# The gate and the embeddings' product of a decoder trunk, rearranged: another order of the seven gate products and of their banks, the residual added by accumulating transfers, and three quarters of the embeddings' product moved into the hand-ordered second phase

## The chip, the core and the metric

The kernel runs on one core of one Trainium2 chip. The metric is the device time of one execution in microseconds (us). Before the change the median of three executions is 2514.31 us (2514.18 to 2516.86).

## What is computed

One layer of a decoder trunk, all in float32, with 2048 tokens and a model width of 1024:

```python
u = rmsnorm(h, ln1_g);  proj = u @ w_in          # gated linear attention + short convolution
h = h + concat([o, y]) @ w_out
u2 = rmsnorm(h, ln2_g);  a, bb = split(u2 @ w_gate_upffn)
h = h + (silu(a) * bb) @ w_down                  # hidden width 2816
u3 = rmsnorm(h, ln3_g)
gate = sigmoid(u3 @ w_ple_gate)                  # 1024 x 1024
h = h + gate * (p @ w_ple_proj)                  # p: 2048 x 256, the "embeddings"
return rmsnorm(h, lnf_g)
```

The change touches the last three lines of the sum: the gate, and the product `p @ w_ple_proj`.

## The kernel before

**Arithmetic.** Each float32 operand of a product is split into a high part (a cast on ACT, line 161) and a low part (a subtraction on DVE, line 162). A product is three matmul passes: high x high, high x low, low x high (`PASSES`, `product` at line 143, matmul at line 147). A "cut" below is such a cast with its subtraction. The big products (up, down, gate) use a seven-product scheme in the manner of Strassen: a 2 x 2 block product is formed from seven products of sums of blocks, numbered 1 to 7, whose results are combined.

**First phase, `mixing_phase` (line 284).** Four blocks of 512 tokens, `NB` of them, each with `NT` = 4 tiles of 128 tokens. `block` (line 639) does norm, input projection, attention, convolution and, for two column halves `n` and four tiles `ti`, the output projection (`unit`). After the second half of each tile, `norm_to_ops` (line 219) forms the second norm, turns it (`tr`, line 202), copies the turned tile from PSUM on ACT (line 233), fetches four older operand blocks from HBM (line 231), forms the sums for the seven products with four subtractions on POOL (line 217) and stores them to `up_ops` (line 234). In this phase only PE's order is written by hand; the other engines' instructions are ordered by the scheduler. At its end stands `embedding` (line 699): first `load_U` (line 713) for the first four products of the next phase, which fetches their operands (line 268) and cuts them, then all of `p @ w_ple_proj`: `p` is turned in four blocks of 512 tokens (line 708), each followed by 8 products of 6 matmuls, whose results ACT copies from PSUM (line 726) and SP stores as 16 tiles `emb` (line 728).

**Second phase, `up_phase` (line 771).** Gate-up products, every engine in the order in which the code is written, from a table of due work that `run(g)` carries out (groups -6 to -1 are run before the first product, lines 864 to 867).

**Last phase, `last_phase` (line 947).** Also in written order. `stream` (line 1010) works through a list of jobs of two steps each; a step is 12 matmuls (line 1022). Raw operands `wr` and `mr` are loaded four jobs ahead (line 981) and cut into `wh` and `mh` two jobs ahead (lines 161 and 162). `then(n, fn)` puts work off by `n` steps. First comes `down` for two batches of 1024 tokens, then `gated(0)` and `gated(1)` (line 1161). All seven gate products take 4 steps each. SP issues all transfers in order, and each of them first waits for the transfer issued eight earlier and for its buffers. PSUM has four banks `ps0` and four `ps1`; a product either opens four banks of its own or goes on in those of an earlier one (`stream(..., on, ...)`).

In `gated` before: the order is 1, 6, 2, 5, 7, 3, 4. Product 1 is copied to `acc`, 6 is added to `acc` by DVE, 2 goes on in 1's banks, 3 in 5's and 4 in 7's. `onto` (line 1178) multiplies the gate by the embedding tile `pp` (buffer pool of 4, fetched by SP at line 1172) and adds it to the row `h`: the addition, in part also the multiplication, is on POOL (line 217). The rows `h` are loaded by SP (line 1153), three when the half begins and five at step 10. `finish` norms a row (squares on ACT at line 1060, the inverse root on POOL at lines 1064 and 1066, scaling on DVE at line 1079) and stores it (line 1185). In the last half product 4 is done token tile by token tile, with `last_done4` (line 1254): `early_half` multiplies by the norm's gain on POOL, and the scaled copies of `late_half` are on POOL (line 1211) for four tiles and on ACT (line 1209) for the other four.

Of the kernel before, what the change touches and what calls it, by code (L numbers as in the profile page):

```python
# [8 lines left out]
F32 = mybir.dt.float32  # L9
F32R = mybir.dt.float32r  # L10
# [28 lines left out]
def hybrid_layer(ctx: ExitStack, tc: tile.TileContext,  # L39
# [212 lines left out]
    def load_x(b, ti, eng, gate=None):  # L252
        xt = w4([P, D])
        r = b * T + ti * P
        d = eng.dma_start(out=xt, in_=x[r:r + P, :])
        if gate is not None:
            after(d, gate)
        return xt

# [24 lines left out]
    def mixing_phase(st):  # L284
# [354 lines left out]
        def block(b, u1, first):  # L639
# [7 lines left out]
            for n in range(2):  # L647
# [3 lines left out]
                for ti in range(NT):  # L651
# [10 lines left out]
                    unit(ps, uT_at(mix, tok_of(ti)), wo, NK, o_done)  # L662
            return u1
# [27 lines left out]
        pts = []  # L691

        def embedding_loads():
            for q in range(2):
                pts.append(w4([P, NT, 256]))
                r = slice(q * T, (q + 1) * T)
                nc.sync.dma_start(out=pts[q], in_=p[r, :].rearrange("(t p) d -> p t d", p=P))

        def embedding():
            wp = [weights(w_pp, [(n * 512, 512)], 0, 2) for n in range(2)]  # L700

            def turned(q):
                pT = [w4([P, 2, T], F32R) for _ in range(2)]
                for j in range(2):
                    tp = tr_bank().rearrange("p (k t) -> p k t", k=2)
                    for k in range(2):
                        for i in range(2):
                            nc.tensor.transpose(out=tp[:, k, i * P:(i + 1) * P],
                                                in_=pts[q][:, 2 * j + i, k * P:(k + 1) * P], identity=ident)
                    sl = slice(j * 256, (j + 1) * 256)  # L710
                    split_into(pT[0][:, :, sl], pT[1][:, :, sl], tp)
                return pT
            for n in ORDER[:4]:
                load_U(0, n, last["h"])
            pT = turned(0)
            for q in range(NB):
                if q + 2 < NB:
                    pts.append(w4([P, NT, 256]))
                    r = slice((q + 2) * T, (q + 3) * T)
                    nc.sync.dma_start(out=pts[q + 2], in_=p[r, :].rearrange("(t p) d -> p t d", p=P))  # L720
                for ti in range(NT):
                    o = w4([P, D])
                    for n in range(2):
                        ps = mm_bank()
                        product(ps, lambda k, s: pT[s][:, k, tok_of(ti)], wp[n], 2)
                        nc.scalar.copy(out=o[:, n * 512:(n + 1) * 512], in_=ps)
                        tick()
                    nc.sync.dma_start(out=emb[q * NT + ti], in_=o)
                    if ti == 1 and q + 1 < NB:
                        nxt = turned(q + 1)  # L730
                pT = nxt
# [39 lines left out]
    def up_phase(st):  # L771
# [175 lines left out]
    def last_phase(st):  # L947
# [14 lines left out]
        jobs = [(kind, b, n, i) for kind in range(2) for b in range(NBB) for n in ORDER  # L962
# [47 lines left out]
        def stream(kind, b, n, bk, on, done, by_token=False):  # L1010
            nk = kinds[kind][3]
            if on is None:
                tag = f"ps{flip[0] if n in (1, 7) else 1 - flip[0]}"
# [147 lines left out]
        def gated(b, lnf, final):  # L1161
            h = rows_of(h_out, b, 10)
            acc = [v("acc") for _ in range(NT)]
            bk, x22 = {}, [None] * NT
            part = [tiny.tile([P, 1], F32, name="part", bufs=2 * NT) for _ in range(2 * NT)] if final else None

            pp = {}

            def fetch(tiles, cols):
# [178 lines left out]
```

## Time and profile before

| | |
|---|---|
| median of three executions | 2514.31 us |
| the profiled execution | 2518.72 us |
| its span, first to last instruction | 2517.0 us |
| granted TensorE clock, mean | 0.979 |
| PE busy | 2388.6 us (95%) |
| DVE busy | 1405.2 us (56%) |
| ACT busy | 965.9 us (38%) |
| POOL busy | 775.1 us (31%) |
| moved by DMA | 470.03 MB, 187 GB/s in the mean |

The profiled execution is 4.41 us longer than the median, and 1.72 us of it lie around the span. The profile names an instruction by engine, line, operation and tiles ("mm<-hl,w" is a product into bank `mm` from `hl` and `w`). "Busy" is the sum of the durations. Behind an idle stretch stands in brackets its length and what released the engine: "[8.87 <-ACT mh L161]" is 8.87 us of waiting that a cast of `mh` on ACT ended. SPq is SP's queue of transfer issues, and "to landing" is the time from a transfer's issue until its data are there. Windows and timelines count in us from the span's start. The first phase ends and the second begins at about 1013 us, and the gate runs from about 2293 us to the end.

### The profile page before, as it was taken

The numbers are of one execution on the slowest core, as the hardware profiler recorded it, in microseconds if no ns is written. First come the engines' busy times: TensorE is split into PE (matmuls) and PEld (weight loads), VectorE is DVE, ScalarE is ACT, GpSimd is POOL, SyncE is SP. The second block draws the span as 40 slices with busy tenths as digits, with TensorE's granted clock in tenths as the row PEclk, the third lists the DMA queues.
The fourth block names the chain that finished last, engine by engine and source line by source line (L and its number), as shares of the span: only waits on it lengthen the run. The fifth ranks groups of instructions, "written<-read, shape, count | busy, mean of one in ns | idle before, by whom it ended". The sixth has DMA issues, their size and how long they took to land.

```text
span 2517.0 us, 31414 instructions
## 1 busy us (share of the span) xinstructions
PE 2388.6 (95%) x11752; PEld 1950.2 (77%) x11752; DVE 1405.2 (56%) x1662; ACT 965.9 (38%) x1511; POOL 775.1 (31%) x636
## 2 busy tenths in 40 slices
PE   7999999899999986999999999999999999999885
PEld 6777878777887765788888888888878887888664
DVE  4655465466537532555555754444546555656587
ACT  4434433353344324422222522222233354335454
POOL 3301211430103022334434144335413005303577
PEclk9999999999999998999999999999999999999888
DMA  4226323731442168635435666567677569658884
GB/s 152 67 68 225 95 68 143 221 107 61 167 126 76 60 205 296 222 135 179 159 134 184 221 250 217 194 225 259 234 246 242 190 225 358 207 198 291 296 306 162
DMA packets 273065, 470.03 MB, mean 187 GB/s; under 512 B 22528, under 2 KB 145936, under 8 KB 272912
## 3 DMA queue, kind: packets, MB, share of 16 engines
q1 hardware_dynamic: 272720, 468.00, 55.1%
q8 instruction: 92, 1.51, 0.2%
q14 instruction: 61, 0.50, 0.1%
q0 software_dynamic: 192, 0.02, 0.0%
HBM read 325.87 MB, written 142.08 MB: 186 GB/s over the span
## 4 chain that ended last, share of the span: by engine, by line
PE 66%; DMA 5%; POOL 3%; DVE 3%; ACT 2%; issue 1%; SPq 1%; DVEq 0%; POOLq 0%; ACTq 0%
PE mm L147 48%; PE ps L1022 16%; DMA mr<-u 1%; PE g L415 1%; DMA raw<-up 1%; DMA mr<-hid 1%; POOL h L217 1%; DVE mh L162 1%; DMA h<-h_out 0%; DMA wr<-in_w_ple_gate_dram 0%; DVE wh L162 0%; POOL w L217 0%; POOL as L217 0%; DVE g L217 0%; ACT mh L161 0%
## 5 line engine op out<-in xcount | busy, mean ns | idle before, releaser
L1022 PE MATMUL ps<-wh,mh 128*128 128x512 f32 x2520 | 592.5, 396 | 31.1 <-ACT mh L161 14.7
L1022 PEld LDWEIGHTS ps<-wh,mh 128*128 128x128 f32 x2520 | 478.8, 191 | 138.9 <-ACT mh L161 16.3
L147 PE MATMUL mm<-uT,hl 128*128 128x512 f32 x1920 | 481.8, 405 | 10.6 <-DVE hl L105 6.7
L147 PE MATMUL mm<-uT,wu 128*128 128x512 f32 x2112 | 482.7, 389 | 2.1 <-ACT wu L161 1.6
L147 PEld LDWEIGHTS mm<-uT,wu 128*128 128x128 f32 x2112 | 396.2, 188 | 85.2 <-ACT wu L161 2.1
L147 PEld LDWEIGHTS mm<-uT,hl 128*128 128x128 f32 x1920 | 356.8, 190 | 105.4 <-DVE hl L105 12.0
L147 PE MATMUL mm<-U,wu 128*128 128x512 f32 x1584 | 362.6, 389 | 0.0
L147 PEld LDWEIGHTS mm<-U,wu 128*128 128x128 f32 x1584 | 297.3, 188 | 61.7
L162 DVE TENSOR_TENSOR wu<-raw,wu 128x1024 fp32r<-128x1024 f32 x154 | 213.8, 1390 | 225.3 <-ACT wu L161 225.3
L147 PE MATMUL mm<-hl,uT 128*128 128x512 f32 (+1 forms) x1488 | 278.9, 347 | 3.4 <-DVE uT L162 2.1
L161 ACT CAST wu<-raw 128x1024 fp32r<-128x1024 f32 x154 | 161.3, 1049 | 307.2 <-PE mm L147 235.5
L162 DVE TENSOR_TENSOR wh<-wr,wh 128x1024 fp32r<-128x1024 f32 x112 | 149.2, 1332 | 224.7 <-ACT wh L161 224.6
L147 PEld LDWEIGHTS mm<-hl,uT 128*128 128x128 f32 x1488 | 235.2, 191 | 39.2 <-DVE uT L162 2.7
L217 DVE TENSOR_TENSOR v<-mm,v 128x512 f32<-128x512 f32 x220 | 151.3, 688 | 160.0 <-PE mm L147 159.2
L217 POOL TENSOR_TENSOR v<-v,v 128x512 f32<-128x512 f32 x88 | 139.9, 1590 | 303.1 <-DMA hid<-v 286.1
L161 ACT CAST wh<-wr 128x1024 fp32r<-128x1024 f32 x112 | 111.9, 999 | 272.2 <-PE ps L1022 186.9
L105 DVE TENSOR_TENSOR hl<-raw,hl 128x512 fp32r<-128x512 f32 (+1 forms) x260 | 183.3, 743 | 28.7 <-ACT hl L104 28.5
L104 ACT CAST hl<-raw 128x512 fp32r<-128x512 f32 (+1 forms) x260 | 154.0, 623 | 66.4 <-PE mm L147 34.2
L217 POOL TENSOR_TENSOR raw<-raw 128x1024 f32<-128x1024 f32 x44 | 106.1, 2423 | 217.6 <-issue 159.3
L162 DVE TENSOR_TENSOR mh<-mr,mh 128x1024 fp32r<-128x1024 f32 x112 | 153.9, 1374 | 6.6 <-ACT mh L161 6.3
L161 ACT CAST mh<-mr 128x1024 fp32r<-128x1024 f32 x112 | 111.5, 996 | 11.7 <-DMA mr<-hid 9.0
L217 POOL TENSOR_TENSOR ur<-ur 128x512 f32<-128x512 f32 x60 | 92.8, 1547 | 31.0 <-DMA ur<-in_w_ple_gate_dram 26.1
(173 smaller groups left out, 1968.0 us busy)
## 6 DMA issues: line engine op xcount, KB each, us to landing
raw<-in_w_gate_upffn_dram SPq DMA_DIRECT2D x77, 512.0 KB, 4.5
hid<-v SPq DMA_DIRECT2D x154, 256.0 KB, 3.4
mr<-hid SPq DMA_DIRECT2D x70, 512.0 KB, 4.8
raw<-in_w_in_dram SPq DMA_DIRECT2D x64, 512.0 KB, 4.6
wu<-raw SPq DMA_DIRECT2D x44, 512.0 KB, 2.8
raw<-wu SPq DMA_DIRECT2D x44, 512.0 KB, 5.7
wr<-wd SPq DMA_DIRECT2D x40, 512.0 KB, 3.7
w<-in_x_dram SPq DMA_DIRECT2D x32, 512.0 KB, 8.5
```

The lines of the kernel that those rows point to most:

```text
L104: nc.scalar.copy(out=hl[:, 0, :], in_=raw)
L105: nc.vector.tensor_tensor(out=hl[:, 1, :], in0=raw, in1=hl[:, 0, :].bitcast(F32), op=ALU.subtract)
L147: nc.tensor.matmul(out=out_ap, lhsT=lhs(k, a), rhs=rhs(k, b), start=(start and k == 0 and i == 0), stop=(k == nk - 1 and i == 2), **kw)
L161: nc.scalar.copy(out=hi, in_=src)
L162: nc.vector.tensor_tensor(out=lo, in0=src, in1=hi.bitcast(F32), op=ALU.subtract)
L217: return e.tensor_tensor(out=out, in0=a, in1=b, op=op)
L415: nc.tensor.matmul(out=sp[par][:, a, :], lhsT=X[r, c], rhs=X[r, c], start=True, stop=True)
L1022: nc.tensor.matmul(out=bk[n][t], lhsT=M[:, a, j, tok_of(t)], rhs=W[:, c, j, :], start=(on is None and k == 0 and i == 0), stop=(k == nk - ...
```

## The change

**Embeddings.** Only the first block of `p` (512 tokens) stays in the first phase. It is turned by `embedding_turned` behind the second tile of the last output projection, and its 8 products stand at the phase's end. The four `load_U` are gone from there. The other three blocks (24 products of 6 matmuls) stand at the start of the hand-ordered second phase: `p` is loaded into `ur` tiles, `w_ple_proj` is loaded and cut a second time (two transfers of 512 KB), and a table `events` puts the fetches and cuts of the operands of the first gate-up products, and the groups -6 to -1 of due work, between the 24 products. The results are stored as 24 transfers of 256 KB, each three products late.

**Gate.** The order is 1, 2, 6, 5, 7, 3, 4. Product 6 goes on in 1's banks, then 7 and 4 do too, and 3 goes on in 5's. 12 instead of 20 results are added up by DVE in each half, and product 4's sigmoid reads PSUM itself. In `gated(0)` `onto` is a single multiplication on DVE that writes `h`, and the old row is added by a transfer that POOL issues with `accum_op=add` (`residual`, eight of 512 KB); the squares come two steps after it. The embedding tiles come half in `pp` and half in `ut` buffers. In `gated(1)` all eight rows are loaded at step 8, and `onto`, `early_half` (both on DVE) and the scaled copies (on ACT) no longer use POOL. On POOL there remain the small inverses and the eight issues.

```diff
@@ embedding, first phase
+        def embedding_turned():
+            hi_lo = [w4([P, 2, T], F32R) for _ in range(2)]
+            turned_p(emb0["p"], lambda s, sl: hi_lo[s][:, :, sl], tr_bank)
...
-            for n in ORDER[:4]:
-                load_U(0, n, last["h"])
-            pT = turned(0)
-            for q in range(NB):
...
+            for ti in range(NT):
+                o = w4([P, D])
+                for n in range(2):
+                    ps = mm_bank()
+                    product(ps, lambda k, s: emb0["pT"][s][:, k, tok_of(ti)], emb0["w"][n], 2)
...
@@ up_phase
-        for g in range(-6, 0):
-            run(g)
-        load_U(0, ORDER[4])
-        side += fetch_U(0, ORDER[5])
+        for q in range(1, NB):
+            pts.append(pl["ur"].tile([P, 2, T], F32, name="ur"))
...
+        events = {0: lambda: (fetch_next(0), run(-6), run(-5), run(-4)), 3: lambda: (cut_all(), fetch_next(1)),
...
+                    events.get(u, lambda: None)()
+                    ps = mm_bank()
+                    product(ps, lambda k, s: pT(q)(k, s)[:, tok_of(ti)], lambda k, s: wpp[:, 2 * n + k, s, :], 2)
+                    o = v2()
+                    nc.scalar.copy(out=o, in_=ps)
...
@@ last_phase
-        jobs = [(kind, b, n, i) for kind in range(2) for b in range(NBB) for n in ORDER
+        orders = [ORDER, (1, 2, 6, 5, 7, 3, 4)]
+        jobs = [(kind, b, n, i) for kind in range(2) for b in range(NBB) for n in orders[kind]
...
@@ gated
+                if not final:
+                    tensor(V, row(t)[:, cols], sg, pp[t, cols.start], ALU.mult)
+                    return
+                tensor(V, sg, sg, pp[t, cols.start], ALU.mult)
+                tensor(V, h[t][:, cols], h[t][:, cols], sg, ALU.add)
...
             def finish(t, start):
-                norm_steps(h[t], lnf, start, (1, 2), lambda got: then(start + 3, lambda: store(t, got["xn"])))
+                def residual():
+                    nc.gpsimd.dma_start(out=h[t], in_=h_out[b * 2 * NT + t], accum_op=ALU.add)
+                then(start, residual)
+                norm_steps(h[t], lnf, start + 2, (1, 2), lambda got: then(start + 5, lambda: store(t, got["xn"])))
...
-                tensor(G, h[t][:, cols], h[t][:, cols], lnf[:, cols], ALU.mult)
+                tensor(V, h[t][:, cols], h[t][:, cols], lnf[:, cols], ALU.mult)
...
             def done4(t, x):
-                z = v("g")
-                tensor(V, z, x, acc[t], ALU.add)
-                then(1, lambda: sigmoid(z, z))
-                then(2, lambda: onto(t, hi, z, V, G))
-                finish(t, 4 + t)
+                z = v("acc")
+                sigmoid(x, z)
+                then(1, lambda: onto(t, hi, z))
+                then(1, lambda: finish(t, 2 + t))
...
+            if final:
+                then(8, lambda: [row(t) for t in range(2 * NT)])
+            then(1, lambda: fetch(early, lo, "pp"))
+            go(1, None, done1)
+            go(2, None, done2)
+            go(6, 1, done6)
             go(5, None, done5)
-            go(7, None, done7)
+            then(1, lambda: fetch(late, hi, "ut"))
+            then(3, lambda: fetch(late, lo, "pp"))
+            go(7, 1, done7)
+            then(1, lambda: fetch(early, hi, "ut"))
             go(3, 5, done3)
...
+            go(4, 1, last_done4 if final else done4, by_token=final)
```

**ACT at the end of the first phase, before.** `w<-tr` is the copy of a turned tile of the second norm, `uT<-raw` a cast of an operand for the next phase, and `w<-mm` the copy of a result of the embeddings' product.

```order
L178 ACTIVATE w_7932,ss<-w_7574 128x1024
L233 COPY w_7940<-tr 128x512 x2
L161 CAST w_8018<-tr 128x2x256 x2
L161 CAST uT<-raw 128x2x512 x6
L726 COPY w_8036<-mm 128x512
L161 CAST uT<-raw 128x2x512
L726 COPY w_8036<-mm 128x512
L161 CAST uT<-raw 128x2x512
L233 COPY w_8053<-tr 128x512 x2
L726 COPY w_8080<-mm 128x512 x2
L161 CAST w_8098<-tr 128x2x256 x2
L726 COPY w_8114<-mm 128x512 x2
```

**The same place after.** `U_8133` to `U_8135` hold the split blocks of `p` and `w_ple_proj` in the second phase.

```order
L178 ACTIVATE w_7962,ss<-w_7574 128x1024
L233 COPY w_7970<-tr 128x512 x2
L722 COPY w_7996<-mm 128x512 x2
L233 COPY w_8013<-tr 128x512 x2
L722 COPY w_8040<-mm 128x512 x2
L722 COPY w_8058<-mm 128x512 x2
L722 COPY w_8076<-mm 128x512 x2
L161 CAST U_8134<-raw 128x2x512 x2
L161 CAST U_8133<-mm 128x2x256 x4
L161 CAST U_8135<-mm 128x2x256 x2
L900 COPY v_8203<-mm 128x512
L900 COPY v_8212<-mm 128x512
```

The eight casts `uT<-raw` stood ahead of the copies of the last turned tile and are now behind them, among the 24 later copies.

**SP at the same place, before:** the stores of the last tile's sums (`up`), the loads of `p` and the stores of `emb`.

```order
L268 DMA raw<-up_5_105 128x1024 x2
L720 DMA w_8034<-in_p_dram 128x4x256
L231 DMA w_8054<-up_1_109 128x4x128
L231 DMA w_8054<-up_2_111 128x4x128
L728 DMA emb_196<-w_8036 128x1024
L234 DMA up_3_114<-w_8053 512x1x128
```

**SP after:**

```order
L234 DMA up_4_115<-w_8014 512x1x128
L724 DMA emb_196<-w_7996 128x1024
L724 DMA emb_197<-w_8040 128x1024
L724 DMA emb_198<-w_8058 128x1024
L724 DMA emb_199<-w_8076 128x1024
L862 DMA ur<-in_p_dram 128x4x256 x3
L866 DMA raw<-in_w_ple_proj_dram 128x2x512 x2
L279 DMA ur<-up_1_102 128x1024 x2
```

The loads of `p` for the second block of tokens stood ahead of the last stores of the first phase, and those of the last three blocks now stand behind the last tile's stores and behind the four stores of `emb`.

**POOL in `gated(0)`, before:** row additions (`h<-h,g`, `h<-h,x`) and multiplications (`g<-g,pp`), then the small inverses.

```order
L217 TENSOR_TENSOR g<-g,pp 128x512
L217 TENSOR_TENSOR h<-h,g 128x512
L217 TENSOR_TENSOR h<-h,x 128x512 x4
L217 TENSOR_TENSOR h<-h,g 128x512 x4
L1064 TENSOR_SCALAR ms<-ss_18227 128x1
L1066 TENSOR_TENSOR rs<-ms,mhalf 128x1
L1064 TENSOR_SCALAR ms<-ss_18254 128x1
```

**POOL after:**

```order
L1246 DMA h<-h_out_90 128x1024
L1246 DMA h<-h_out_91 128x1024
L1246 DMA h<-h_out_92 128x1024
L1106 TENSOR_SCALAR ms<-ss_18250 128x1
L1108 TENSOR_TENSOR rs<-ms,mhalf 128x1
L1246 DMA h<-h_out_93 128x1024
L1106 TENSOR_SCALAR ms<-ss_18296 128x1
```

POOL's row work is gone, and the transfers of the residual stand in POOL's queue among the inverses.

More of the change, by code (lines that the diff above doesn't have):

```diff
@@ L258, in load_x, with turned_p @@
         return xt
+    def turned_p(src, dst, bank):
+        for j in range(2):
+            tp = bank().rearrange("p (k t) -> p k t", k=2)
+            for k in range(2):
+                for i in range(2):
+                    nc.tensor.transpose(out=tp[:, k, i * P:(i + 1) * P],
+                                        in_=src[:, 2 * j + i, k * P:(k + 1) * P], identity=ident)
+            sl = slice(j * 256, (j + 1) * 256)
+            split_into(dst(0, sl), dst(1, sl), tp)
     U = [{}, {}]
@@ L662, in block @@
                     unit(ps, uT_at(mix, tok_of(ti)), wo, NK, o_done)
+                    if not more and n == 1 and ti == 1:
+                        embedding_turned()
             return u1
@@ L688, in start @@
                         fill_mask(L)
-        pts = []
+        emb0 = {}
         def embedding_loads():
[L694 to L697, printed above, removed]
-        def embedding():
[L700 to L712, printed above, removed]
-            for n in ORDER[:4]:
-                load_U(0, n, last["h"])
-            pT = turned(0)
-            for q in range(NB):
[L717 to L731, printed above, removed]
@@ new lines, in up_phase, with pT @@
+        for n in range(2):
+            nc.sync.dma_start(out=wpp_raw[n], in_=w_pp[:, n * 512:(n + 1) * 512].rearrange("(k p) n -> p k n", p=P))
+        spare2 = [pl["U2"].tile([P, 4, 2, T], F32R, name="U2") for _ in range(3)]
+        wpp = spare2[1]
+        for n in range(2):
+            split_into(wpp[:, 2 * n:2 * n + 2, 0, :], wpp[:, 2 * n:2 * n + 2, 1, :], wpp_raw[n])
+        def pT(q):
+            t = spare2[0 if q < 3 else 2]
+            return lambda k, s: t[:, (q - 1) % 2 * 2 + k, s, :]
@@ new lines, in up_phase @@
+        stores = []
+        u = 0
+        for q in range(1, NB):
+            for ti in range(NT):
+                for n in range(2):
+                    events.get(u, lambda: None)()
[3 more added lines that the diff above has]
+                    nc.scalar.copy(out=o, in_=ps)
+                    stores.append((emb[q * NT + ti][:, n * 512:(n + 1) * 512], o))
+                    if len(stores) > 2:
+                        nc.sync.dma_start(out=stores[0][0], in_=stores[0][1])
+                        stores.pop(0)
+                    u += 1
@@ L868, in up_phase @@
+        for d, o in stores:
+            nc.sync.dma_start(out=d, in_=o)
+        side += cuts
         for b in range(NBB):
@@ L1223, in done5, with done6 @@
+            def done6(t, x):
+                u2[t] = v("g")
+                nc.scalar.copy(out=u2[t], in_=x)
             def done5(t, x):
-                x22[t] = v("x")
-                tensor(V, x22[t], x, acc[t], ALU.add)
+                p5[t] = v("x")
+                nc.scalar.copy(out=p5[t], in_=x)
             def done7(t, x):
-                tensor(V, x22[t], x, x22[t], ALU.add)
-                then(1, lambda: sigmoid(x22[t], x22[t]))
-                then(2, lambda: onto(NT + t, hi, x22[t], V, G))
@@ L1231, in done7 @@
[L1231 to L1232 removed]
+                z = p5[t]
+                tensor(V, z, x, z, ALU.add)
+                then(1, lambda: sigmoid(z, z))
+                then(2, lambda: onto(NT + t, hi, z))
                 if final:
[L1234 removed]
+                    then(3 + t // 2, lambda: early_half(NT + t, hi))
             def done3(t, x):
[L1237 to L1238 removed]
+                z = u2[t]
```

126 lines of the change are left out of this document (71 added, 55 removed).

## The prediction

> **What bounds the kernel now.** I read the page first, then the waits of PE, then the windows, then the timelines of the two stretches that the windows single out. The page's busy times:
>
> ```profile
> span 2517.0 us, 31414 instructions
> PE 2388.6 (95%) x11752; PEld 1950.2 (77%) x11752; DVE 1405.2 (56%) x1662; ACT 965.9 (38%) x1511; POOL 775.1 (31%) x636
> ```
>
> PE is busy for 95% of the span. The change leaves the number of matmuls as it is, so what it can gain lies in PE's 128 us of idle time (2517.0 - 2388.6) and in matmuls that run slowly behind a stall. The windows show where these lie (PE busy and its count, ..., clock, DMA share, GB/s):
>
> ```profile
> 900.00:950.00 50.00, 40.10 (x184) 31.85 (x182) 18.14 (x22) 15.11 (x26) 18.29 (x20) 0.93 0.57 173
> 950.00:1000.00 50.00, 32.27 (x146) 26.62 (x147) 12.54 (x13) 24.54 (x39) 12.13 (x7) 0.80 0.88 301
> 1050.00:1100.00 50.00, 50.00 (x222) 41.38 (x222) 29.91 (x30) 13.86 (x17) 22.73 (x12) 1.00 0.50 168
> 2300.00:2350.00 50.00, 48.25 (x226) 39.34 (x225) 29.91 (x23) 24.38 (x34) 36.20 (x24) 1.00 1.03 348
> 2350.00:2400.00 50.00, 36.02 (x139) 27.61 (x137) 34.04 (x31) 18.97 (x24) 22.55 (x15) 0.86 0.77 258
> 2400.00:2450.00 50.00, 40.26 (x148) 30.97 (x149) 42.59 (x34) 27.52 (x40) 33.20 (x25) 0.86 0.87 316
> 2450.00:2517.00 67.00, 37.66 (x164) 30.34 (x162) 52.29 (x51) 29.94 (x56) 49.97 (x39) 0.82 0.47 176
> ```
>
> An undisturbed stretch (1050 to 1100) runs 222 matmuls in 50 us, or 0.225 us each; that is my full rate. The boundary of the first two phases and the gate fall well below it, and both are what the change touches.
>
> **The boundary.** PE's timeline there:
>
> ```profile
> 932.16 1.14 PE L708 MATMUL tr<-ident,w 128*128 128x128 f32 x8 [1.56 <-ACT w L233]
> 933.53 0.73 PE L147 MATMUL mm<-hl,w 128*128 128x512 f32 x2 [0.23 <-ACT w L161]
> 940.36 3.99 PE L147 MATMUL mm<-hl,w 128*128 128x512 f32 x10 [6.09 <-DVE w L162]
> 967.73 1.97 PE L708 MATMUL tr<-ident,w 128*128 128x128 f32 x8 [19.74 <-ACT w L233]
> 1012.62 0.73 PE L147 MATMUL mm<-uT,wu 128*128 128x512 f32 x2 [1.62 <-ACT wu L161]
> 1013.88 1.42 PE L147 MATMUL mm<-uT,wu 128*128 128x512 f32 x5 [0.52 <-DVE wu L162]
> ```
>
> Idle in all: 1.56 + 0.23 + 6.09 + 19.74 + 1.62 + 0.52 = 29.8 us. The long one ends with a copy on ACT (L233). ACT's own timeline says why that copy is late:
>
> ```profile
> 946.23 1.05 ACT L161 CAST uT<-raw 128x1024 fp32r<-128x1024 f32 x1 [12.26 <-DMA raw<-up]
> 966.15 1.05 ACT L161 CAST uT<-raw 128x1024 fp32r<-128x1024 f32 x1 [1.70 <-DMA raw<-up]
> 967.10 1.07 ACT L233 COPY w<-tr 128x512 f32<-128x512 f32 x2
> ```
>
> ACT stood in the casts of the next phase's operands, eight of them from 946 to 967, each waiting for its transfer, and the copy that frees PE's `tr` bank stood behind them.
>
> **The gate.** Its 2 x 7 x 4 x 12 = 672 matmuls, counted back from the last one in PE's timeline, begin 13 matmuls into its first row, at 2292.7, and the second half begins 22 matmuls into the fifth, at 2390.2:
>
> ```profile
> 2289.78 24.87 PE L1022 MATMUL ps<-wh,mh 128*128 128x512 f32 x109
> ...
> 2362.46 19.08 PE L1022 MATMUL ps<-wh,mh 128*128 128x512 f32 x73 [8.87 <-ACT mh L161]
> ...
> 2384.47 12.28 PE L1022 MATMUL ps<-wh,mh 128*128 128x512 f32 x47 [1.71 <-DVE mh L162]
> ...
> 2416.51 0.80 PE L1022 MATMUL ps<-wh,mh 128*128 128x512 f32 x1 [4.01 <-DVE wh L162]
> ...
> 2480.26 9.36 PE L1022 MATMUL ps<-wh,mh 128*128 128x512 f32 x40 [1.72 <-DVE mh L162]
> ```
>
> PE ends at 2480.26 + 9.36 = 2489.6. So the halves take 97.5 and 99.4 us where 336 matmuls at full rate are 75.6, and the tail to 2517.0 takes 27.4. The waits are for cuts. Cuts are late for two reasons, which SP's waits (in 2240 to 2517), the lines by form (from 2290) and DVE's timeline show:
>
> ```profile
> SPq L1172 <- DVE x L217: 22.3, 8, 10.0
> SPq L1172 <- DVE g L217: 19.6, 8, 7.0
> ```
>
> ```profile
> L162 DVE TENSOR_TENSOR mh<-mr,mh 128x1024 fp32r<-128x1024 f32 x27 | 45.8, 1695 | 1.4 <-ACT mh L161 1.3
> L162 DVE TENSOR_TENSOR wh<-wr,wh 128x1024 fp32r<-128x1024 f32 x27 | 43.3, 1603 | 40.8 <-ACT wh L161 40.8
> L217 POOL TENSOR_TENSOR h<-h,g 128x512 f32<-128x512 f32 x20 | 35.4, 1788 | 15.4 <-DVE g L217 14.7
> ```
>
> ```profile
> 2469.95 1.22 DVE L162 TENSOR_TENSOR mh<-mr,mh 128x1024 fp32r<-128x1024 f32 x1
> 2477.92 2.29 DVE L162 TENSOR_TENSOR mh<-mr,mh 128x1024 fp32r<-128x1024 f32 x1
> ```
>
> First, the embedding fetches wait 42 us in SP's queue for `pp` buffers, and the raw loads stand behind them. Second, a cut takes DVE 1.22 us while POOL is idle (2469.95) and 2.29 while POOL adds rows (2477.92). The Trainium skill, page "SBUF — State Buffer", section "SBUF: two separate sides", says the same of its cause: an exclusive lock on a port pair, which a DVE operation with two SBUF inputs and a GpSimd operation that reads SBUF take in turns. The trace agrees, 2.29 against 1.22.
>
> **The change part by part.** Durations are of the profiled execution (2518.72 us, span 2517.0, 1.72 around it), which is 4.41 us over the median; I take the differences from it and put them on the median.
>
> *Boundary.* The casts of operands go behind the copies. The last turned tile's own norm still holds PE for about as long as the first three stalls, some 5 to 8 us, and the first block's products end at about 950. Then the path is SP: the second block of `p` is issued behind the stores of the last tile, whose sums on POOL come one tile every 10.5 us:
>
> ```profile
> 932.37 2.61 POOL L217 TENSOR_TENSOR w<-w,w 128x512 f32<-128x512 f32 x2 [4.50 <-DMA w<-up]
> ...
> 942.87 2.63 POOL L217 TENSOR_TENSOR w<-w,w 128x512 f32<-128x512 f32 x2 [4.48 <-DMA w<-up]
> 946.71 1.29 POOL L217 TENSOR_TENSOR w<-w,w 128x512 f32<-128x512 f32 x1
> ```
>
> At that pace the last tile's sums run from 953.4 and take 5.1 us (946.71 + 1.29 - 942.87) to 958.5, and `p` is issued at about 959. The landings over the whole kernel were
>
> ```profile
> w<-in_p_dram SPq DMA_DIRECT2D x4, 512.0 KB, 9.2
> raw<-in_w_ple_proj_dram SPq DMA_DIRECT2D x2, 512.0 KB, 7.4
> ```
>
> so `p` is there at 968 and turned and cut two or three us later; 144 matmuls at 0.225 are 32.4 us, 34 with a slow start, which gives 1004 to 1005 for the first up product against 1012.6: **-8 us**. The table adds two transfers of the weight, and ACT has the eight casts among its 24 copies; eight `mm` banks of 6 matmuls (8 x 1.35 = 10.8 us) cover those. Bounds: +2 if the loads come 10 us later, -14 if SP is not held by the last tile.
>
> *First half of the gate.* The eight row loads leave it: 4.2 MB, at the 348 GB/s of the saturated window 12 us of transfer. The waits for `pp` go, POOL's row work goes, and the cuts fall from 1.6 to 1.7 us towards 1.22. Of the 21.9 us over full rate some are turns of the last norm, which stay. The 8.87 stall is the one I count, since it stands behind the saturated stretch: **-8**, bounds 0 and -15.
>
> *Residual.* Eight accumulating transfers come in. No row of before shows one. The nearest are the same rows by SP, and three small transfers issued by POOL:
>
> ```profile
> h<-h_out SPq DMA_DIRECT2D x16, 512.0 KB, 6.9
> cw<-in_conv_w_dram POOLq DMA_DIRECT2D x3, 2.0 KB, 3.5
> ```
>
> The squares come two steps (24 matmuls, 5.4 us) later. From 3.5 us up to 13.8 (twice 6.9, if the old row is read and then written) both an early and a late landing are open. I take 7: 1.5 us late, hidden by cuts that are two jobs (10.8 us) ahead. Their 4.2 MB lie in the second half. The Trainium skill, page "DMA: Bandwidth & Descriptors", section "Anatomy of one DMA", fits 2.0 us + bytes/436e3 to a transfer that GpSimd issues, for 512 KB an estimate of 3.2 us; no run here shows it, and the same rows by SP took 6.9. By it the squares would never wait and the sum would stay as it is.
>
> *Second half.* DVE loses 8 additions but takes `onto` and `early_half` from POOL, 24 row operations of 512 columns: at half of a cut's 1.22 us for 1024 columns some 15 us, against 54 cuts in both halves that each lose up to 0.4 us. All eight rows are asked for at step 8, next to stores and the residual, in a half that moved 258 and 316 GB/s in the windows and has the 348 of the first as a measure of room: (348 - 258) x 50 + (348 - 316) x 50 = 6.1 MB, against the 4.2 MB that come. The 23.8 us over full rate shrink by the `pp` waits and shorter cuts, and some stalls for rows appear: **-8**, bounds +8 and -18.
>
> *Tail.* POOL's end, from its timeline:
>
> ```profile
> 2486.02 6.34 POOL L217 TENSOR_TENSOR h<-h,g 128x512 f32<-128x512 f32 x4
> ...
> 2499.35 3.52 POOL L1211 TENSOR_SCALAR w<-h,rs 128x512 f32<-128x512 f32 x2
> ...
> 2503.91 4.15 POOL L1211 TENSOR_SCALAR w<-h,rs 128x512 f32<-128x512 f32 x2
> ```
>
> Additions to 2492.4, then inverses, then scaled copies to 2508: all but the inverses leave POOL. After the last matmul there remain sigmoid, multiplication, addition, squares, inverse and scaling of one tile, about 6 us, and its store, while eight stores (4.2 MB at 348 GB/s, 12 us) begin a little before PE's end: 13 of 27.4 remain, **-14**, bounds -6 and -17.
>
> Sum: -8 - 8 - 8 - 14 = -38 us, so 2514.3 - 38 = 2476 (the profiled execution would be 2481).
>
> **The rivals.**
>
> *The boundary gives nothing.* ACT's casts have only moved among the 24 copies. If operands land late there, in a stretch that already moved 301 GB/s in 950 to 1000 and gets two transfers more, banks fill and PE waits as now. Against it: the fetches are now three products (4 us) ahead of the casts, and the eight banks stand behind that. It gives -30: 2484.
>
> *The gate stays bound by its transfers.* The bytes of the gate are the same, only later, and the burst of rows at step 8 holds DVE (its `onto` waits for a row, with cuts queued behind). For it: 348 GB/s in 2300 to 2350 with a DMA share of 1.03. Against it: the windows behind that one are below. Both halves then give nothing, -8 - 14 = -22: 2492.
>
> *Slower: late residuals.* On POOL's queue the fourth residual stands behind the first row's inverse, which waits for squares, which wait for the first residual; so three are under way at a time. With a landing of L the rows come L/3 apart, where steps are 2.7 us, and ACT stands in the squares ahead of its casts. Over eight rows PE loses 8 x (L/3 - 2.7) + (L - 5.4) less the 10.8 us of cuts ahead: at L = 13.8, 13 us, which leaves 2489; at L = 20 some 35, which eats the gain; at 25 about 53, which gives 2530. It decides from L = 20, three times the 6.9 of SP's rows. For it: the operation has no row here, and it falls into the stretch where SP's own stores bunch. Against it: that factor.
>
> *The change does not do what it says.* PE's matmuls are the same in number, and if the stalls were set by PE's order alone nothing would move: 2514. Against it stand ACT's casts and POOL's rows above, both visibly ahead of what PE waits for.
>
> **How the numbers follow.** Forecast 0.62; boundary without gain 0.13; gate bound by transfers 0.12; late residuals 0.10; no effect 0.03. A measurement of this kernel can tell about 0.2%, 5 us, from no change. All of the first three are faster by more; of late residuals 0.08 are slower by more and 0.02 in between: faster 0.87, same 0.05, slower 0.08. The terms' bounds reach from 2514.3 - 14 - 15 - 18 - 17 = 2450 up, but will not all fall on one side; two thirds of the way down from the forecast is 2459. Above, the range takes in the second rival, 2492, with some of its own spread: 2502. Left out are the late residuals, no effect and about 0.05 at the ends.
>
> **What would show it.** Right: no wait of PE on ACT L233 above 7 us around 950, the first up product near 1004; cuts in the gate near 1.22 to 1.3 us; PE's end at about 2462 to 2466 and a tail of 12 to 14 us. Wrong: squares on ACT released by the residual's transfer with waits over 8 us; DVE's `onto` released by `h<-h_out`; a wait of PE at 950 that is as long as before and only ends with `p`; a tail over 20 us.

## The result and the profile after

The changed kernel takes 2490.27 us (median of four, 2487.02 to 2492.85) against 2515.59 us for the kernel before: the ratio is 0.9897, with a 95% interval from 0.988 to 0.9914. That is faster by 1.0%, as forecast, and inside the forecast range, but by 25 us and not by 38. One execution of the run "rows by SP" below took 8366 us and is left out of its median.

The span of the profiled execution fell from 2517.0 to 2488.0 us. Its pieces follow from PE's timeline, by counting the gate's 672 matmuls back from the last one as the prediction did (the middle of the gate falls inside a row of many matmuls and is taken there in proportion; the starts of the single matmuls would move it by 0.6 to 0.7 us in these two kernels and by at most 1.5 in the runs below, from one half to the other):

| us | before | after | difference | forecast |
|---|---|---|---|---|
| first up product | 1012.6 | 1008.5 | -4.1 | -8 |
| beginning of the gate | 2292.7 | 2285.8 | -6.9 | |
| first half of the gate | 97.5 | 85.8 | -11.7 | -8 |
| second half | 99.4 | 99.3 | -0.1 | -8 |
| tail, PE's end to the span's end | 27.4 | 17.1 | -10.3 | -14 |

In the runs below that share the changed kernel's code up to that point, the first up product came between 1003.6 and 1009.7 us, so the first two rows are good to a few us; the halves and the tail repeat within some 2 us where their code is the same. The pieces add up to 29.0 us and not to 25.3, since the profiled execution of the kernel before lay 3.1 us above its median and that of the change 0.6 below.

**The boundary** in PE's timeline of the changed kernel:

```profile
940.40 1.94 PE L202 MATMUL tr<-ident,w 128*128 128x128 f32 x8 [3.88 <-DVE w L195]
941.99 10.61 PE L147 MATMUL mm<-hl,w 128*128 128x512 f32 x36
964.67 5.35 PE L266 MATMUL mm<-ident,ur 128*128 128x128 f32 x24 [12.07 <-DMA ur<-in_p_dram]
971.80 0.73 PE L147 MATMUL mm<-U,U 128*128 128x512 f32 x2 [1.77 <-ACT U L161]
1008.49 6.74 PE L147 MATMUL mm<-uT,wu 128*128 128x512 f32 x29
```

The wait of 19.74 us for a copy behind ACT's casts is gone. In its place PE waits 12.07 us for `p`. The wait that ends last before the products is a shorter one for ACT, which had waited for the weight:

```profile
969.09 2.17 ACT L161 CAST U<-raw 128x1024 fp32r<-128x1024 f32 x2 [15.87 <-DMA raw<-in_w_ple_proj_dram]
971.16 3.02 ACT L161 CAST U<-mm 128x512 fp32r<-128x512 f32 x6
```

The casts of the weight stand ahead of those of the turned `p`, so the weight, which landed at about 969, holds the products at least as much as `p`. From the first of their 144 matmuls to the first up product 36.7 us pass.

**The gate.** PE's timeline shows one long wait in the second half; ACT's timeline shows what it stood in:

```profile
2390.44 5.29 PE L1064 MATMUL ps<-wh,mh 128*128 128x512 f32 x22 [0.63 <-DVE mh L162]
2405.58 1.22 PE L1064 MATMUL ps<-wh,mh 128*128 128x512 f32 x2 [9.86 <-ACT mh L161]
2461.55 9.36 PE L1064 MATMUL ps<-wh,mh 128*128 128x512 f32 x40 [0.63 <-DVE mh L162]
```

```profile
2378.24 1.06 ACT L1102 ACTIVATE w<-h 128x1024 f32<-128x1024 f32 x1 [5.21 <-DMA h<-h_out]
2402.50 1.06 ACT L1102 ACTIVATE w<-h 128x1024 f32<-128x1024 f32 x1 [10.31 <-DMA out_dram<-w]
2404.49 1.04 ACT L161 CAST mh<-mr 128x1024 fp32r<-128x1024 f32 x1
```

The squares of the first row waited 5.21 us for its residual. Those of a later row waited 10.31 us for the store that had to leave its output buffer, and the cast that PE needed stood behind them. The windows (with the clock, the DMA share and the GB/s at the end) and the DMA view from 2375 to 2425 us show what made that store late:

```profile
2330.00:2380.00 50.00, 47.73 (x201) 38.72 (x202) 35.66 (x37) 24.40 (x32) 11.54 (x9) 0.97 1.00 321
2380.00:2430.00 50.00, 36.22 (x141) 27.78 (x140) 32.40 (x34) 26.31 (x42) 14.24 (x20) 0.88 1.00 322
```

```profile
q1 hardware_dynamic: 3397, 11.35, 59.5%
q0 software_dynamic: 1088, 3.93, 40.6%
...
out_dram<-w SPq DMA_DIRECT2D x7, 512.0 KB, 10.1
h<-h_out POOLq DMA_DIRECT2D x5, 512.0 KB, 8.7
...
pp<-emb SPq DMA_DIRECT2D x4, 256.0 KB, 17.2
```

The DMA engines are full for 100 us. The queue of POOL's transfers (q0), the residuals, takes 40.6% of their time for 3.93 MB, which is 10.3% for each MB; SP's queue (q1) takes 59.5% for 11.35 MB, or 5.2% for each MB. Behind it an embedding tile of 256 KB takes 17.2 us to land.

DVE's cuts, in the lines by form from 2285 us on, did get faster, to 1.37 to 1.38 us from 1.60 to 1.70, with POOL's own row work for the gate gone:

```profile
L162 DVE TENSOR_TENSOR mh<-mr,mh 128x1024 fp32r<-128x1024 f32 x27 | 37.2, 1380 | 0.2
L162 DVE TENSOR_TENSOR wh<-wr,wh 128x1024 fp32r<-128x1024 f32 x27 | 37.0, 1370 | 51.9 <-ACT wh L161 51.9
```

**The tail.** DVE's timeline, from its last cut to its last instruction:

```profile
2460.28 1.22 DVE L162 TENSOR_TENSOR mh<-mr,mh 128x1024 fp32r<-128x1024 f32 x1
2461.41 1.28 DVE L217 TENSOR_TENSOR h<-h,gain 128x512 f32<-128x512 f32 x2
...
2470.32 0.68 DVE L217 TENSOR_TENSOR acc<-acc,ut 128x512 f32<-128x512 f32 x1
...
2482.44 0.75 DVE L1266 SCALAR_TENSOR_TENSOR w<-h,rs,gain 128x512 f32<-128x512 f32 x1 [0.84 <-POOL rs L1108]
```

PE is done at 2470.9, and DVE only then comes to the last product's rows: from 2461.4 on it has row work without a pause until 2474, part of it (the additions to `h` and the gain) taken over from POOL.

### The profile page after: what moved, and what is told of

Same layout as the page of the kernel before. It is cut to its first block, busy times and chain, and to the rows that moved or that the text cites. A ratio compares the mean times of both kernels' runs of the same rounds, so it can differ in the third digit from the quotient of the medians.

```text
span 2488.0 us, 31410 instructions
## 1 busy us (share of the span) xinstructions
PE 2385.9 (96%) x11752; PEld 1950.7 (78%) x11752; DVE 1399.8 (56%) x1676; ACT 975.3 (39%) x1533; POOL 694.5 (28%) x596
## 4 chain that ended last, share of the span: by engine, by line
PE 65%; DMA 6%; DVE 3%; ACT 2%; issue 2%; POOL 2%; SPq 1%; POOLq 0%; DVEq 0%; ACTq 0%
PE mm L147 47%; PE ps L1064 15%; DMA mr<-u 1%; DMA mr<-hid 1%; PE g L426 1%; DMA pp<-emb 1%; POOL w L217 1%; DVE mh L162 1%; DMA out_dram<-w 1%; DMA w<-up 0%; DVE h L217 0%; DMA h<-h_out 0%; DVE wh L162 0%; PE ps L1097 0%; ACT mh L161 0%
## 5 line engine op out<-in xcount | busy, mean ns | idle before, releaser
L162 DVE TENSOR_TENSOR wu<-raw,wu 128x1024 fp32r<-128x1024 f32 x154 | 221.4, 1437 | 209.0 <-ACT wu L161 208.9
L162 DVE TENSOR_TENSOR wh<-wr,wh 128x1024 fp32r<-128x1024 f32 x112 | 144.2, 1288 | 231.9 <-ACT wh L161 231.6
L162 DVE TENSOR_TENSOR mh<-mr,mh 128x1024 fp32r<-128x1024 f32 x112 | 146.5, 1308 | 5.4 <-ACT mh L161 5.1
L161 ACT CAST mh<-mr 128x1024 fp32r<-128x1024 f32 x112 | 111.6, 996 | 10.7 <-DMA mr<-hid 9.2
```

The costliest lines, as they stand in the source:

```text
L161: nc.scalar.copy(out=hi, in_=src)
L162: nc.vector.tensor_tensor(out=lo, in0=src, in1=hi.bitcast(F32), op=ALU.subtract)
```

## The experiments

The question is where the second half's forecast gain went, and which parts of the change carried the rest. Two theories run through the expectations. Theory A: the accumulating transfers of the residual ate the second half's gain. Theory B: the gate is bound by its bytes, which the change only moved. All edits are to the changed kernel. Times are medians, ratios are against the kernel before on the same chip; halves and tail are of the profiled execution.

| run | time | ratio, 95% interval | first half | second half | tail |
|---|---|---|---|---|---|
| the change | 2490.27 | 0.9897 (0.988 to 0.9914) | 85.8 | 99.3 | 17.1 |
| rows by SP | 2489.18 | 0.9889 (0.987 to 0.9907) | 92.4 | 94.9 | 15.5 |
| no residual | 2477.85 | 0.9842 (0.9825 to 0.9858) | 84.3 | 90.1 | 16.0 |
| plain copy | 2477.43 | 0.9845 (0.9827 to 0.9863) | 84.8 | 90.3 | 17.1 |
| squares apart | 2487.29 | 0.9876 (0.9861 to 0.9891) | 84.5 | 97.1 | 17.1 |
| copied and apart | 2490.64 | 0.9886 (0.9871 to 0.9902) | 88.1 | 95.7 | 17.6 |
| copied early | 2489.91 | 0.9896 (0.9878 to 0.9914) | 88.8 | 95.2 | 17.6 |
| copied in turn | 2488.3 | 0.9884 (0.9867 to 0.9902) | 84.4 | 96.2 | 17.6 |
| old boundary | 2496.87 | 0.9918 (0.9902 to 0.9934) | 84.0 | 100.3 | 17.0 |
| `p` by ACT | 2493.03 | 0.991 (0.9885 to 0.9936) | 84.6 | 99.9 | 17.7 |
| all in `pp` | 2500.7 | 0.9935 (0.992 to 0.9949) | 84.6 | 109.3 | 17.1 |
| idle rows on POOL | 2513.98 | 0.9982 (0.9972 to 0.9992) | 94.3 | 114.3 | 18.6 |
| gain on POOL | 2492.87 | 0.9896 (0.9881 to 0.991) | 84.1 | 106.4 | 14.3 |

**The residual left out.**

```diff
-                def residual():
-                    nc.gpsimd.dma_start(out=h[t], in_=h_out[b * 2 * NT + t], accum_op=ALU.add)
-                then(start, residual)
```

> The changed kernel without the eight accumulating transfers: the old row of the first 1024 tokens is left out of the sum, everything else is as before. Theory A and B both expect the second half to lose its 9.9 us stall, about 2480. If the stall comes from the stores and their four buffers alone, the time stays within 3 us of 2490.

Measured: 2477.85 us, the second half 90.1. The residual transfers cost 12 us by the medians and 14 by the ratios (0.0055 of 2516); in the profiled executions 9.2 us of it lie in the second half, 1.5 in the first and 1.1 in the tail.

The output of this run, and of the next one, is not the layer's: here the old row is missing, there it overwrites the gate's product.

**The residual as a plain copy.**

```diff
-                    nc.gpsimd.dma_start(out=h[t], in_=h_out[b * 2 * NT + t], accum_op=ALU.add)
+                    nc.gpsimd.dma_start(out=h[t], in_=h_out[b * 2 * NT + t])
```

> The same eight transfers, on the same queue, with the same waits and bytes, but copying instead of accumulating, so the gate's term of the first 1024 tokens is left out (overwritten). Theory A, in the form that the accumulation itself costs DMA time: about 2482, and the share of the software queue for 4.2 MB falls from 9.5% of the window to about 5%. Theory B, bytes and queue: 2490, the share stays.

Measured: 2477.43 us, the same as with no transfer at all, and the second half 90.3. The DMA view from 2360 to 2410 us, first of the changed kernel, then of this one, holds all eight transfers in both:

```profile
q0 software_dynamic: 1151, 4.19, 45.1%
...
out_dram<-w SPq DMA_DIRECT2D x5, 512.0 KB, 12.0
...
pp<-emb SPq DMA_DIRECT2D x4, 256.0 KB, 17.2
```

```profile
q0 software_dynamic: 1152, 4.19, 21.3%
...
out_dram<-w SPq DMA_DIRECT2D x7, 512.0 KB, 7.5
...
pp<-emb SPq DMA_DIRECT2D x4, 256.0 KB, 8.6
```

The same bytes on the same queue take 45.1% of 50 us, or 22.6 us of all engines, when they accumulate and 21.3%, or 10.7 us, when they copy. The difference, 11.9 us, is about the size of the loss: 13 us timed, 9.0 of it in the second half. Theory A holds in its strong form: not the bytes, not POOL's queue and not the waits cost the second half its gain, but the accumulation, where the DMA engines were already full. Why an accumulating transfer takes the engines' time twice, these runs don't show.

**The rows by SP, as in the second half.**

```diff
-                then(start, residual)
...
+            else:
+                then(5, lambda: [row(t) for t in range(3)])
+                then(10, lambda: [row(t) for t in range(3, 2 * NT)])
```

> The gate's first half takes its old rows by plain transfers on SP (three rows five steps and five rows ten steps after the half begins) and adds them on DVE, as the second half does; no accumulating transfer is left. Theory A, the accumulating transfers ate the second half's gain: they took 10.3% of the DMA engines' time for each MB between 2375 and 2425 us against 5.2% for the others, delayed the squares and through them the stores and cuts. Then the second half falls from 99.3 us to some 90, the first grows by 0 to 3, and the time is about 2481 to 2485. Theory B, the gate is bound by the bytes alone: the 4.2 MB only move back into the first half, which grows by about 10 us, and the time is 2490 to 2495.

Measured: 2489.18 us; the first half grew by 6.6 us to 92.4, the second fell by 4.4 to 94.9. Neither theory had both: the second half is relieved, but by half of what A expected, and the first pays for its rows, 6.6 us of the 10 that B expected. Its window shows the transfers full there again:

```profile
2330.00:2380.00 50.00, 43.13 (x166) 33.61 (x165) 35.89 (x38) 21.34 (x28) 8.51 (x5) 0.90 1.01 348
```

So having the 4.2 MB of rows, and their additions on DVE, out of the first half is worth 6.6 of its 11.7 us.

**The squares apart from the output buffer.** In `finish` the squares write into a tile `as`, and the output tile is taken at the scaling.

```diff
+                    sq = pl["as"].tile([P, 2, 4, P], F32, name="as")
+                    squares(h[t], sq.rearrange("p a b c -> p (a b c)"), got["ss"])
...
+                    got["xn"] = w4([P, D])
```

> The changed kernel, but in the first half of the gate the squares write into a scratch tile, and the output tile (one of four) is taken two steps later, at the scaling; the accumulating transfers stay. If the stall in the second half comes from squares that wait for the store of an earlier row to leave its buffer (ACT waited 10.3 us for that in the changed kernel), the half falls from 99.3 us to about 91 and the time to about 2481. If it comes from the slow accumulating transfers, which delay the raw loads and the stores alike, the wait moves from ACT to DVE's scaling and the time stays within 4 us of 2490.

Measured: 2487.29 us; the second half is 97.1 and has lost 2.2 of the 9 us in question. ACT's waits in the gate say where the rest stands:

```profile
ACT as L1102 <- DMA h<-h_out: 15.0, 8, 5.5
```

ACT now waits eight times for the residuals, 15.0 us in all, where the changed kernel had four such waits of 8.9 us and the one of 10.31 for a store, which is gone. The buffer was the place where the loss showed, not its cause.

**The old rows copied and added by DVE.** Three forms of it, with complete outputs; the first two differ in when POOL issues the copies.

```diff
+                    got0["old"] = pl["as"].tile([P, 2, 4, P], F32, name="as").rearrange("p a b c -> p (a b c)")
+                    nc.gpsimd.dma_start(out=got0["old"], in_=h_out[b * 2 * NT + t])
+                then(start, residual)
+                then(start + 2, lambda: tensor(V, h[t], h[t], got0["old"], ALU.add))
```

> The old rows of the first half come by the same POOL transfers, but copied into scratch tiles and added by DVE (eight additions of 1024 columns); the squares write into that scratch tile and the output tile is taken at the scaling. The output is complete. Theory A (accumulating costs the DMA engines twice the time): the second half is near 91 us and the time about 2476 to 2480, as in the run that only copied (2477.4). If DVE's added 10 us come out on PE's path, 2483 to 2488.

Measured: 2490.64 us. The second half improved to 95.7, but the first rose to 88.1. POOL's timeline shows that nothing held the first copies back any more:

```profile
2338.36 1.75 POOL L1249 DMA_DIRECT2D as<-h_out  x3
```

They went out at 2338 instead of 2370, in the stretch that has no room. One step earlier in the program, but ahead of an inverse in POOL's queue:

> As the run that copied the old rows into scratch tiles and let DVE add them, but each copy is issued one step earlier, ahead of an inverse that stood before it in POOL's queue. If that queue and the four scratch tiles throttled the rows there (the squares came 3 to 7 us apart where steps are 2.7), the second half falls from 95.7 towards 91 us and the time to 2481 to 2485. If DVE's eight added operations are the cost, the time stays at 2487 to 2491.

Measured: 2489.91 us, halves of 88.8 and 95.2: no difference, so that queue was not what held the second half. The last form makes each copy wait for the row's last product on DVE:

```diff
-                    nc.gpsimd.dma_start(out=got0["old"], in_=h_out[b * 2 * NT + t])
+                    after(nc.gpsimd.dma_start(out=got0["old"], in_=h_out[b * 2 * NT + t]), gates[t])
```

> The old rows are copied into scratch tiles and added by DVE, as in the two runs before it, but each copy now waits for the row's last product on DVE, as the accumulating transfer did; in those two the first copies went out some 30 us earlier, into the saturated first half, which took 88 us instead of 85.8. The output is complete. Theory A: the first half returns to 85, the second lies between the 90.3 of plain copies without an addition and 95.7, and the time is 2481 to 2486. If the copies cost the same wherever they stand and DVE's additions are the rest, the second half grows to 97 or more and the time stays at 2488 to 2491.

Measured: 2488.3 us. The first half is back at 84.4, as theory A says, but the second is 96.2 and not near 90. In ACT's waits

```profile
ACT as L1102 <- DVE h L217: 23.4, 11, 5.9
```

the squares now wait for DVE's additions, which stand in order among the cuts. These waits suggest that the addition gives back on DVE and ACT what the plain copy saved on the DMA engines; they do not show how much of it reached PE. No form with a complete output beats the change by more than these runs can tell: the intervals of this one and of the squares apart overlap with the change's.

**The old boundary with the new gate.** The first two phases are those of the kernel before.

```diff
-        def embedding_turned():
...
+            for n in ORDER[:4]:
+                load_U(0, n, last["h"])
```

> The new gate with the old embeddings' product, all of it in the first phase. By the two traces the first up product came 4.1 us earlier and the gate 6.9 us earlier. If the boundary is worth what the traces show, the time is 2494 to 2497. Rival: the boundary is worth the forecast 8 us, 2498. Rival: it is worth nothing, since the gate's transfers set the end, 2490.

Measured: 2496.87 us, 0.9918. Against the change that is 0.0021 of 2516 us, about 5 us for the boundary; the intervals of the two ratios overlap, and it agrees with the 4.1 us of the traces. In this run's trace the first up product came at 1015.0 us, 2.4 later than in the kernel before with the same boundary. In the eleven traces with the new boundary and `p` issued by SP it came at 1007.5 in the mean, 5.1 and 7.5 us ahead of the two with the old one, so the single pair of traces understates the term.

**`p` and its weight issued by ACT.**

```diff
-            nc.sync.dma_start(out=pts[-1].rearrange("p a t -> p (a t)").rearrange("p (t d) -> p t d", t=NT),
+            nc.scalar.dma_start(out=pts[-1].rearrange("p a t -> p (a t)").rearrange("p (t d) -> p t d", t=NT),
```

> The changed kernel with the second phase's loads of the embeddings and their weight issued by ACT instead of SP. By the trace ACT is done with its copies at 953.2 us, and SP issued them from 958.1 to 962.6 behind the last tile's stores. If SP's order is what PE's 12.1 us wait rests on, the wait falls to about 7 to 8 us, the first up product comes at about 1004 and the time falls by 4 to 5 us to about 2486. If the transfers or their buffers are bound elsewhere, nothing changes: 2490.

Measured: 2493.03 us. ACT did issue at 953.45, 4.6 us before SP did, but PE's timeline has

```profile
958.63 1.94 PE L266 MATMUL mm<-ident,ur 128*128 128x128 f32 x8 [6.65 <-DMA ur<-in_p_dram]
965.37 1.97 PE L266 MATMUL mm<-ident,ur 128*128 128x128 f32 x8 [4.80 <-DMA ur<-in_p_dram]
969.04 1.97 PE L266 MATMUL mm<-ident,ur 128*128 128x128 f32 x8 [1.71 <-DMA ur<-in_p_dram]
973.76 1.22 PE L147 MATMUL mm<-U,U 128*128 128x512 f32 x2 [2.75 <-ACT U L161]
```

The first block lands earlier, the second and third do not, and the products begin at 973.8 instead of 971.8. ACT's timeline has the reason:

```profile
970.48 1.04 ACT L161 CAST U<-raw 128x1024 fp32r<-128x1024 f32 x1 [17.88 <-DMA raw<-in_w_ple_proj_dram]
972.18 1.04 ACT L161 CAST U<-raw 128x1024 fp32r<-128x1024 f32 x1 [0.66 <-DMA raw<-in_w_ple_proj_dram]
973.13 3.02 ACT L161 CAST U<-mm 128x512 fp32r<-128x512 f32 x6
```

The weight was asked for at 957.5 instead of 961.4 and was there for its casts at 970.5 instead of 969.1, and the casts of the turned `p` stand behind it. So an earlier issue did not bring the data earlier. That the transfers around it (the last tile's stores, `emb`, `p` itself) held it is argued from the DMA share of 0.93 in 950 to 1000 us of the changed kernel; no run shows it.

**All embedding tiles in one pool.**

```diff
-            then(1, lambda: fetch(late, hi, "ut"))
+            then(1, lambda: fetch(late, hi, "pp"))
```

(The other `"ut"` likewise.)

> The changed kernel with all embedding tiles fetched into the one pool of four, as before the change, instead of half of them into another pool: SP waits for its buffers again, with the raw loads behind it. If these waits (42 us in SP's queue before) held the gate, each half grows by 3 to 8 us: 2496 to 2505. If SP had slack, the time stays within 3 us of 2490.

Measured: 2500.7 us, 10.4 us more, all of it in the second half (109.3). SP's waits in the gate have the old ones back:

```profile
SPq L1220 <- DVE h L217: 17.5, 10, 9.3
SPq L1220 <- DVE g L217: 10.8, 4, 8.0
SPq L1220 <- DVE x L217: 9.7, 4, 6.9
```

**Idle rows on POOL.**

```diff
+            def row_on_pool():
+                for c in (0, 256):
+                    tensor(G, idle_row, lnf[:, c:c + 256], lnf[:, 512 + c:768 + c], ALU.mult)
```

> The changed kernel with idle work on POOL: beside each of the 32 row steps and 8 gain steps of the gate, two products of 256 columns of the gain tile into a scratch tile that nothing reads, about as much POOL time as before the change. Nothing waits for it but POOL's own inverses and transfers. If POOL's row work slowed DVE's cuts (1.65 us each before, 1.37 after), the cuts return to about 1.6 us and the halves grow by 3 to 10 us: 2494 to 2502. If the cuts' slowness cost PE nothing, the time stays within 3 us of 2490.

Measured: 2513.98 us, 0.9982: work that nothing reads takes back 24 us by the medians and 21 by the ratios (0.0085 of 2516), nearly the whole gain. Both halves grow, by 8.5 and 15.0 us. The lines by form from 2285 us, a cut in DVE's timeline beside the idle products, and one of ACT's waits in the gate:

```profile
L217 POOL TENSOR_TENSOR idle<-gain 128x256 f32<-128x256 f32 x80 | 93.8, 1173 | 5.6
L162 DVE TENSOR_TENSOR mh<-mr,mh 128x1024 fp32r<-128x1024 f32 x27 | 41.5, 1536 | 0.0
L162 DVE TENSOR_TENSOR wh<-wr,wh 128x1024 fp32r<-128x1024 f32 x26 | 39.4, 1516 | 50.5 <-ACT wh L161 50.5
```

```profile
2327.09 1.76 DVE L162 TENSOR_TENSOR wh<-wr,wh 128x1024 fp32r<-128x1024 f32 x1
```

```profile
ACT x L1296 <- DMA u<-x: 16.1, 2, 9.9
```

The cuts are 0.15 us longer in the mean, 53 x 0.15 = 8 us on DVE, and a single one beside the idle products takes 1.76 us against 1.22 alone. The other part is POOL's own queue: the idle products stand ahead of the last norm's subtractions, so the stores of `u` come late, and ACT waits 16.1 us for them ahead of its casts, where the changed kernel's trace has no such wait and that of "gain on POOL" one of 5.3 us. The run doesn't tell the two apart; how the loss divides between them stays open.

**The gain on POOL.**

```diff
-                tensor(V, h[t][:, cols], h[t][:, cols], lnf[:, cols], ALU.mult)
+                tensor(G, h[t][:, cols], h[t][:, cols], lnf[:, cols], ALU.mult)
```

> The changed kernel, but the eight multiplications by the gain in the last half are on POOL again, as before the change; 5.1 us of DVE go. If DVE's queue sets the tail (it runs without a gap from 2459 to 2475 us), the tail falls from 17.1 to about 14 and the time to 2486 to 2488. If POOL's work slows DVE's as it did before the change, or the stores set the tail, it stays at 17 and the time at 2490 or a little above.

Measured: 2492.87 us, which the ratios (0.9896 and 0.9897) do not tell from the change. In the profiled execution the tail falls by 2.8 to 14.3, so DVE's queue has a part in it; but the second half grows by 7.1 to 106.4. Beside POOL's products DVE is slow again:

```profile
2424.03 1.79 DVE L217 TENSOR_TENSOR acc<-acc,pp 128x512 f32<-128x512 f32 x1
2461.38 2.30 DVE L162 TENSOR_TENSOR wh<-wr,wh 128x1024 fp32r<-128x1024 f32 x1
```

The same operations take 0.68 and 1.22 us in the changed kernel. In this execution the eight row operations on POOL cost more beside the cuts than they saved behind them.

## Why the prediction was right, and where it was wrong

*Boundary, -8.* The mechanism was right: the wait behind ACT's casts went, and SP issued `p` at 958.1 where 959 was forecast. The term measured -4.1 in the pair of traces, about -5 timed and -5.1 to -7.5 by the mean of eleven traces. The part that was mis-sized is "34 with a slow start" for the 144 matmuls: they took 36.7 us, in a window (950 to 1000 us) with a granted clock of 0.83. The path before them was another than the one told: `p` landed at 964.7, three us earlier than forecast, and the products began at 971.8, about when forecast, because ACT cast the weight first, which the prediction left out of the path. SP's order was not what held them either: with `p` and the weight issued some 4 us earlier the products began no earlier. No run asks for the weight ahead of `p`.

*First half, -8.* Measured -11.7. The single long stall went, as forecast; the run with the rows back in it puts 6.6 us on the rows with their additions. The waits for `pp`, which the prediction counted here too, were worth nothing in this half: with all tiles in `pp` it is 84.6.

*Residual, "1.5 us late, hidden by cuts".* This is the step that failed. The landing was well guessed (8.7 us against 7), and it was the wrong thing to price. The transfers' cost is the time that they hold the DMA engines, 22.6 us for 4.2 MB against 10.7 for a copy, in a stretch that was already full. The prediction counted their 4.2 MB once against 6.1 MB of room and found that they fit; at twice the time for each byte they do not. This term was put at nothing and cost some 13 us.

*Second half, -8.* Measured -0.1. With copies in the place of the accumulations (an incomplete output) it was 90.3 us, -9.1 against before: the term was right, and the residual took it.

*Tail, -14.* Measured -10.3. POOL's additions and scaled copies are gone as forecast; the step that was mis-sized is "about 6 us" after the last matmul for one tile, which took DVE as free. DVE had row work, in part taken over, from 2461.4 to 2483.2, and with the gain back on POOL the tail was 14.3.

*The rivals.* "The gate stays bound by its transfers" came true in the second half, at a DMA share of 1.00 in two windows, though by the price of the residual rather than by the burst of rows. "Late residuals" had the right culprit and the wrong mechanism: by its formula a landing of 8.7 us costs nothing, since 8 x (8.7/3 - 2.7) + 3.3 is less than the 10.8 us of cover, and yet these transfers cost some 13 us. They had chances of 0.12 and 0.10.

*Luck in the total.* The residual's 13 us are as large as the gap from 38 to 25, and 2477.4 us with copies is close to the 2476 forecast, but that is in part chance: the boundary and the tail fell short by 3.9 and 3.7 us in the traces, and the first half gave 3.7 more. Of the signs named beforehand, the long wait on ACT L233 did go, but the cuts (1.37 to 1.38 us), PE's end (2470.9) and the tail (17.1) missed their ranges. PE's wait did end with `p`, though at 12 us and not at 20; no square waited over 5.2 us for a residual and no `onto` of DVE for a row.

*POOL and `pp`.* That POOL's row work held the cuts and the embedding fetches held the raw loads was argued from rows only; the two runs that put them back took 24 and 10 us by the medians. The parts add up to more than the change gained, so they overlap. The Trainium skill, page "SBUF — State Buffer", section "Who interferes with whom", lets a DVE instruction with two SBUF inputs contend with a GpSimd instruction that reads SBUF; the trace agrees, with 1.76 us for a cut beside the idle products and 1.22 without.

## What to carry to other kernels

Price a transfer in a stretch where the DMA engines are full by the time that it holds them, not only by when it lands: the residual's landing looked harmless, and the stall came out three steps on, at an output buffer that a store had not yet left. Work taken off a slow engine is worth what it was holding up, here in two ways, its neighbour's instructions and, it seems, its own queue; check both before giving that engine anything back, however idle it looks. When a wait is released by a buffer, ask what made the buffer late before adding buffers.

## What the runs showed of the hardware

- An accumulating transfer from HBM into SBUF took 2.1 times the DMA engines' time of a copy of the same bytes on the same queue (22.6 us against 10.7 us for 4.19 MB), while its median landing was only 8.7 us against 7.0.
- While the accumulations ran, transfers on the other queue were held up as well: a 256 KB fetch landed in 17.2 us against 8.6 beside plain copies, a 512 KB store in 12.0 against 7.5.
- Three transfers on POOL's queue that no longer had to wait for DVE went out at 2338 us instead of 2370, as soon as POOL came to them, into a stretch (2330 to 2380 us) with a DMA share of 0.97; the half that they landed in took 88.1 us instead of 85.8.
- A transfer that was asked for earlier in a full stretch did not land earlier: the embeddings' weight, issued by ACT at 957.5 us instead of by SP at 961.4, was there at 970.5 instead of 969.1.
- A DVE subtraction of 128x1024 from and into SBUF took 1.22 us alone, 1.76 beside POOL products of 256 columns and 2.3 beside POOL's row work of 512 columns.
